# Seven products for pairs in the output projection and in the fourth quarters, with sums added by accumulating DMAs

## The chip, the cores and the metric

The kernel runs on one core of a Trainium2 chip. The metric is the device time of one execution in microseconds; for each kernel the median of several runs is given. Beside them one execution was recorded by the hardware profiler, and all rows below are of that one.

## The reference

A two-layer decoder trunk on 256 positions with model width 2048, all in float32. Each sub-layer is h = h + RMSNorm_post(f(RMSNorm_pre(h))). What matters here:

```python
def short_conv_mixer(u, w_in, conv_w, w_out):          # layer 0
    proj = u @ w_in                                     # 2048 -> 3 * 2048
    xin, gate_c, gate_b = jnp.split(proj, 3, axis=-1)
    v = gate_c * xin
    ...
    conv = sum(conv_w[k] * vp[:, k:k + S] for k in range(CONV_WIDTH))
    return (gate_b * conv) @ w_out                      # the output projection, 2048 -> 2048

def sq_relu_mlp(u, w_up, w_down):                       # after each mixer
    return jnp.square(jax.nn.relu(u @ w_up)) @ w_down   # 2048 -> 8192 -> 2048
```

Layer 0 is the gated convolution and an MLP; then one shared K and V is made; layer 1 is a stick-breaking attention with 16 heads (query projection, attention, its own output projection) and a second MLP.

## The kernel before

**Precision.** TensorE runs on float32r operands. Every float32 operand is split into a high part, rounded by ACT (`whi`, L145), and a low part, the remainder made by VectorE (`wlo`, L156). One product is then three matmuls: high with high, high with low, low with high (L282, L283, L284).

**The weight stream.** All weights come in one stream of chunks of 128x1024, 512 KB, loaded by SyncE's queue into four buffers (tag raw) and split into a ring of seven pairs of tiles (RING = 7). ACT may write the next ring tile when TensorE has finished with the one seven places earlier.

**Projections with the activations as the stationary operand.** The output projections, K, Q, V and the down projections of the MLPs work in groups of 1024 output columns. A `Group` goes over its chunks i (128 rows of the weight each) and for each chunk over two blocks b of 128 positions and two halves c of 512 columns, into four PSUM banks; a chunk is 12 matmuls of 128x512. After the last chunk the four banks are evicted. The last few chunks of a stage are taken in another order (`last_units`), so that the norm that follows can begin early.

**Seven products.** A `Mixed` group takes some neighbouring chunks i and i + 1 as a pair, a 2x2 block product by a seven-multiplication scheme. `seven` (L349 to L351) does 7 x 3 matmuls for the pair where two ordinary chunks do 8 x 3. Three products (`acc`) go straight into banks of the group; four (p1, p5, p6, p7, the tiles `more`) are kept in four further banks over all pairs of the group and combined once, after its last pair. Each pair needs

- four sums of weight blocks (`split_seven`, VectorE, L182, 128x512 each), in one tile of tag gpre with one buffer, and the split of a, b, t and u, 3.5 chunks' worth in four ring tiles, where two ordinary chunks take two;
- four sums of activation blocks (`sums_of`, L912) and their split (`two_parts`).

**The MLPs.** The hidden width is done in four quarters q. In each, `up` makes 16 hidden tiles, then two down groups j add to the results `part` (tiles `mg`). PAIRS names the pairs of each quarter and group: 2 + 2 in the fourth. In the first three quarters the four kept products are copied out by ACT (L1006) and added to the results by nine accumulating DMAs from GpSimd's queue (L998), once the group is evicted. In the fourth quarter `combined` (L1020 on) forms the four combinations in the middle of the group and VectorE adds them to the results:

```python
            def combine(p1, p5, p6, p7):
                w = pool.tile([P, 4, 512], F32, tag="gpre", name="more", bufs=1)
                t, u2, u3, u4 = (w[:, m, :] for m in range(4))
                nc.scalar.activation(t, p1[:], AF.Copy)                      # L1022
                nc.vector.tensor_tensor(u2, t, p6[:], op=ALU.add)            # L1023
                ...
                for r, v in zip(rs, (t, u4, u3, u2)):
                    nc.vector.tensor_tensor(r, r, v, op=ALU.add)             # L1029
```

At the end of the group `add` adds each bank to its result (L993) and hands it to the norm `after.post` (square on ACT, gain on VectorE at L441).

**The output projection of layer 0** follows the convolution and is two ordinary groups (`project`); their banks go to `mix0.post`. The tile gpre holds, from the stage's start, the gain row of the norm ahead of the MLP.

**What sets the order.** TensorE's order is written out by hand. VectorE, ACT and the DMA queues are ordered by a scheduler when the program is built, with some operations given priority; near the end of a stage (`begin` to `over`) VectorE's and ACT's order is also by hand. Each engine runs its queue in order: an instruction that waits holds back all behind it.

Of the kernel before, what the change touches and what calls it, by code (L numbers as in the profile page):

```python
# [14 lines left out]
P = 128  # L15
# [53 lines left out]
def trunk(ctx, tc, x, xT, vecs, rows, ws, out):  # L69
# [31 lines left out]
    def bank(i, name):  # L101
        return psum.tile([P, 512], F32, tag=f"b{i}", name=name)
# [119 lines left out]
    def part_of(xs, k, b, i):  # L222
        return xs[k // 4][:, k % 4, i, b, :]
# [152 lines left out]
    def tbank():  # L376
        turned["i"] += 1
        return bank(turned["banks"][turned["i"] % 2], "tr")


    h = [const.tile([P, D], F32, name=f"h{b}") for b in range(NB)]
# [331 lines left out]
    mlp_weights(1)  # L713


    def convolution(tmp):
        rot = {"i": -1}

# [67 lines left out]

        y = [None] * 4
        scale = {}

        mean = tmp.tile([P, P], F32, name="mean")  # L790
        nc.vector.memset(mean[:], 1.0 / D)
# [11 lines left out]
        def conv_tile(i, sx, sc, sb):  # L803
            nc.vector.tensor_tensor(sx[:], sx[:], sc[:], op=ALU.mult)
            v = tiny("v", bufs=2, cols=T + 2)
            nc.vector.memset(v[:, :2], 0.0)
            nc.vector.tensor_tensor(v[:, 2:], sx[:], scale["r2"][:], op=ALU.mult)
            c = tiny("conv", bufs=2)
            nc.scalar.activation(c[:], v[:, 2:], AF.Copy, scale=g(G_C2, i))
            nc.vector.scalar_tensor_tensor(c[:], v[:, 1 : T + 1], g(G_C1, i), c[:], op0=ALU.mult, op1=ALU.add)  # L810
            nc.vector.scalar_tensor_tensor(c[:], v[:, :T], g(G_C0, i), c[:], op0=ALU.mult, op1=ALU.add)
            nc.vector.tensor_tensor(sb[:], sb[:], scale["r"][:], op=ALU.mult)
            nc.vector.tensor_tensor(sb[:], sb[:], c[:], op=ALU.mult)
            if y[i // 4] is None:
# [58 lines left out]
    def mlp(pool, i, before, after):  # L873
# [3 lines left out]
        scale = pool.tile([P, T], F32, tag="scale", name="scale", bufs=1)  # L877
        before.spread_to = scale[:]

        def hidden(xs, n, ps, sums, pairs):  # L880
            half = pool.tile([P, T], F32, tag="half", name="half", bufs=2)
            nc.scalar.activation(half[:], ps[:, T:], AF.Copy)
            s = pool.tile([P, T], F32, tag="s", name="s", bufs=3)
            nc.vector.tensor_tensor(s[:], ps[:, :T], half[:], op=ALU.add)
            nc.vector.tensor_tensor(s[:], s[:], scale[:], op=ALU.mult)
            nc.vector.scalar_tensor_tensor(s[:], s[:], 0.0, s[:], op0=ALU.max, op1=ALU.mult)  # L886
            if xs[n // 4] is None:
                xs[n // 4] = operand("hid4")
            if n in pairs and n != APART:
                two_parts([part_of(xs, n, 0, j) for j in range(2)], s[:, :P])  # L890
            else:
                split_tile(xs, n, s[:])
            if n in pairs:
                held[n] = s
            elif n - 1 in pairs:
                sums[n - 1] = sums_of(xs, n - 1, held.pop(n - 1), s)

        def two_parts(parts, src):
            hi, lo = parts
            nc.scalar.activation(hi, src, AF.Copy)  # L900
            nc.vector.tensor_tensor(lo, src, hi.bitcast(F32), op=ALU.subtract)

        def sums_of(xs, n, x, y):

            t = after.dump()
            s1, s2, s3, s4 = (t[:, j * P : (j + 1) * P] for j in range(4))
            a11, a21, a12, a22 = x[:, :P], x[:, P:], y[:, :P], y[:, P:]
            for to, u, v, op in (
                (s1, a21, a22, ALU.add), (s2, s1, a11, ALU.subtract),
                (s3, a11, a21, ALU.subtract), (s4, a12, s2, ALU.subtract),  # L910
            ):
                nc.vector.tensor_tensor(to, u, v, op=op)  # L912
            if n == APART:
                one = pool.tile([P, 2 * P], F32R, tag="s1", name="sums", bufs=1)
                one = [one[:, j * P : (j + 1) * P] for j in range(2)]
            else:
                one = [part_of(xs, n, 1, j) for j in range(2)]
            more = pool.tile([P, 6 * P], F32R, tag="hg", name="sums", bufs=4)
            more = [more[:, j * 3 * P : (j + 1) * 3 * P] for j in range(2)]
            two_parts(one, s1)  # L920
            two_parts(more, t[:, P:])
            return one, more

        def up(q, xs, sums, pairs):
            w = W["up", i, q]
            order = UP_FIRST if q == 0 else UP_ORDER
            place = {kn: m for m, kn in enumerate(order)}
            pss = {}

            def high(k, n, b=None, begin=True, end=False):  # L930

                if n not in pss:
                    pss[n] = bank((n + 2) % 8, "up")
                ps, x = pss[n][:].rearrange("p (a b t) -> p a b t", a=2, b=NB), u[k // 4][:, k % 4]
                if b is None:
                    nc.tensor.matmul(  # L936
                        ps, weight(0, k, n), x, start=begin and k == 0, stop=end and k == KD - 1, skip_group_check=end
                    )
                else:
                    nc.tensor.matmul(ps[:, :, b, :], weight(0, k, n), x[:, :, b, :], start=k == 0 and b == 0, stop=False)  # L940
                if end and k == KD - 1:
                    hidden(xs, n, pss.pop(n), sums, pairs)
                spent(TILE_HIGH if b is None else TILE_LOW)

            def low(k, n, begin=False, end=True):
                if n not in pss:
                    pss[n] = bank((n + 2) % 8, "up")
                x = u[k // 4][:, k % 4, 0].rearrange("p b t -> p (b t)")
                nc.tensor.matmul(  # L949
                    pss[n][:, :T], weight(1, k, n), x, start=begin and k == 0, stop=end and k == KD - 1,  # L950
                    skip_group_check=begin,
                )
                if end and k == KD - 1:
                    hidden(xs, n, pss.pop(n), sums, pairs)
# [62 lines left out]
        def combined(j):  # L1017

            def combine(p1, p5, p6, p7):
# [6 lines left out]
                nc.vector.tensor_tensor(u2, u3, p5[:], op=ALU.add)  # L1026
                rs = [part[b][2 * j + c] for b in range(NB) for c in range(2)]
                for r, v in zip(rs, (t, u4, u3, u2)):
                    nc.vector.tensor_tensor(r, r, v, op=ALU.add)  # L1029
            return combine  # L1030

        for q in range(QUARTERS):
# [21 lines left out]
    def sublayer_pool(name, post, pre):  # L1054
        pool = tc.alloc_tile_pool(name=name, bufs=1, reuse_waits="tile")
        return pool, Norms(pool, row(pool, post, "gpost"), row(pool, pre, "gpre"))
# [262 lines left out]
```

## Time and profile before

| | |
|---|---|
| median of 3 runs | 2144.81 us (2144.78 to 2145.4) |
| the profiled execution | 2144.68 us |
| its span, first to last instruction | 2143.0 us |
| mean granted TensorE clock | 0.999 |
| TensorE busy | 2132.1 us, 99% |
| VectorE, ACT, GpSimd busy | 1649.2, 1241.1, 100.1 us |
| DMA | 445.55 MB, mean 208 GB/s |

The span is what the rows cover; the execution's own time is a little longer. In a row, a line such as L182 is a line of the kernel before; `out<-in` are the tiles written and read; PE is TensorE, DVE is VectorE, POOL is GpSimd. In a row of the timeline the first two numbers are start and duration in microseconds, and brackets tell how long the engine was idle before it and what released it.

### The profile page before, as it was taken

The numbers are of one execution on the slowest core, as the hardware profiler recorded it, in microseconds if no ns is written. First come the engines' busy times: TensorE is split into PE (matmuls) and PEld (weight loads), VectorE is DVE, ScalarE is ACT, GpSimd is POOL, SyncE is SP. The second block draws the span as 40 slices with busy tenths as digits, with TensorE's granted clock in tenths as the row PEclk, the third lists the DMA queues.
The fourth block names the chain that finished last, engine by engine and source line by source line (L and its number), as shares of the span: only waits on it lengthen the run. The fifth ranks groups of instructions, "written<-read, shape, count | busy, mean of one in ns | idle before, by whom it ended". The sixth has DMA issues, their size and how long they took to land.

```text
span 2143.0 us, 29715 instructions
## 1 busy us (share of the span) xinstructions
PE 2132.1 (99%) x10926; PEld 1825.7 (85%) x10926; DVE 1649.2 (77%) x2475; ACT 1241.1 (58%) x1748; POOL 100.1 (5%) x121
## 2 busy tenths in 40 slices
PE   9999999999999999999999999999999999999998
PEld 8888888888888888888888888889888888888886
DVE  7766655898788789678866777558987896887787
ACT  7545444656556556555567888446565565555544
POOL 0000000001101101100000000000011011011000
PEclk9999999999999999999999999999999999999999
DMA  8655664669858858965575545655688588579763
GB/s 305 217 189 186 192 232 146 198 196 263 246 171 255 256 167 245 281 192 175 176 227 166 157 158 177 215 159 167 200 256 259 170 244 267 187 205 268 228 197 124
DMA packets 130321, 445.55 MB, mean 208 GB/s; under 512 B 14592, under 2 KB 14848, under 8 KB 129152
## 3 DMA queue, kind: packets, MB, share of 16 engines
q1 hardware_dynamic: 113472, 408.65, 58.6%
q0 software_dynamic: 16416, 34.61, 8.4%
q8 instruction: 86, 1.41, 0.3%
q14 instruction: 59, 0.48, 0.1%
q10 hardware_dynamic: 288, 0.39, 0.1%
HBM read 413.19 MB, written 2.10 MB: 194 GB/s over the span
## 4 chain that ended last, share of the span: by engine, by line
PE 98%; ACT 1%; DMA 1%; DVE 0%; issue 0%; SPq 0%; DVEq 0%; ACTq 0%
PE up L936 21%; PE acc L282 13%; PE acc L284 13%; PE acc L283 13%; PE up L949 11%; PE acc L758 11%; PE more L350 2%; PE more L349 2%; PE more L351 2%; PE acc L350 2%; PE acc L349 2%; PE acc L351 2%; PE lead L758 1%; PE up L940 1%; PE tr L235 1%; PE z L1092 0%
## 5 line engine op out<-in xcount | busy, mean ns | idle before, releaser
L156 DVE TENSOR_TENSOR wlo<-raw,whi 128x1024 fp32r<-128x1024 f32 (+1 forms) x574 | 687.7, 1211 | 299.5 <-ACT whi L145 244.0
L145 ACT ACTIVATE whi<-raw 128x1024 fp32r<-128x1024 f32 (+1 forms) x574 | 598.1, 1048 | 314.6 <-PE acc L284 135.7
L936 PE MATMUL up<-u,whi 128*128 128x512 f32 x1952 | 458.9, 390 | 0.5 <-ACT scale L517 0.5
L936 PEld LDWEIGHTS up<-u,whi 128*128 128x128 f32 x1952 | 361.6, 188 | 72.3 <-ACT scale L517 0.7
L949 PEld LDWEIGHTS up<-u,wlo 128*128 128x128 f32 x2048 | 256.0, 191 | 5.8
L949 PE MATMUL up<-u,wlo 128*128 128x256 f32 x2048 | 259.0, 283 | 0.0
L282 PE MATMUL acc<-whi,hid 128*128 128x512 f32 x608 | 236.6, 389 | 0.0
L284 PE MATMUL acc<-whi,hid 128*128 128x512 f32 x608 | 236.5, 389 | 0.0
L283 PE MATMUL acc<-wlo,hid 128*128 128x512 f32 x608 | 236.5, 389 | 0.0
L158 DVE SCALAR_TENSOR_TENSOR wlo<-raw,gv,whi 128x512 fp32r<-128x512 f32 (+1 forms) x160 | 132.1, 854 | 42.0 <-ACT whi L145 41.4
L758 PE MATMUL acc<-u,whi 128*128 128x512 f32 x672 | 156.5, 390 | 0.0
L282 PE MATMUL acc<-whi,u 128*128 128x512 f32 x384 | 153.1, 399 | 0.3 <-ACT tk L1162 0.3
L145 ACT ACTIVATE whi<-raw,gv 128x512 fp32r<-128x512 f32 (+1 forms) x160 | 121.8, 800 | 51.8 <-PE acc L284 32.5
L284 PE MATMUL acc<-whi,u 128*128 128x512 f32 x384 | 149.9, 390 | 0.0
L283 PE MATMUL acc<-wlo,u 128*128 128x512 f32 x384 | 149.7, 390 | 0.0
L758 PEld LDWEIGHTS acc<-u,whi 128*128 128x128 f32 x672 | 124.8, 188 | 25.0
L282 PEld LDWEIGHTS acc<-whi,hid 128*128 128x128 f32 x608 | 114.1, 188 | 23.7
L284 PEld LDWEIGHTS acc<-whi,hid 128*128 128x128 f32 x608 | 114.1, 188 | 23.7
L283 PEld LDWEIGHTS acc<-wlo,hid 128*128 128x128 f32 x608 | 114.1, 188 | 23.6
L229 ACT ACTIVATE hid<-s 128x256 fp32r<-128x256 f32 x106 | 44.2, 417 | 135.5 <-DVE s L886 135.1
L998 POOL DMA_DIRECT2D mg<-more x96 | 84.3, 984 | 280.1 <-DMA mg<-more 170.0
L284 PEld LDWEIGHTS acc<-whi,u 128*128 128x128 f32 x384 | 72.1, 188 | 15.4
(2720 smaller groups left out, 3125.3 us busy)
## 6 DMA issues: line engine op xcount, KB each, us to landing
raw<-w_up SPq DMA_DIRECT2D x256, 512.0 KB, 4.5
raw<-w_dn SPq DMA_DIRECT2D x256, 512.0 KB, 4.4
raw<-w_in SPq DMA_DIRECT2D x94, 512.0 KB, 4.0
mg<-more POOLq DMA_DIRECT2D x96, 256.0 KB, 7.4
raw<-w_out SPq DMA_DIRECT2D x32, 512.0 KB, 3.6
raw<-w_v SPq DMA_DIRECT2D x32, 512.0 KB, 4.4
raw<-w_k SPq DMA_DIRECT2D x32, 512.0 KB, 4.3
raw<-w_q SPq DMA_DIRECT2D x32, 512.0 KB, 4.0
```

What stands on the lines that cost most here:

```text
L145: rounded = nc.scalar.activation(hi[:, at], raw[i][:, at], AF.Copy, scale=1.0 if gain is None else gain)
L156: nc.vector.tensor_tensor(lo[:, at], t[:, at], hi[:, at].bitcast(F32), op=ALU.subtract)
L158: nc.vector.scalar_tensor_tensor(lo[:, at], t[:, at], gain, hi[:, at].bitcast(F32), op0=ALU.mult, op1=ALU.subtract)
L282: nc.tensor.matmul(ps[:], xh, hi[:, a], start=i == 0 and k == 0, stop=False)
L283: nc.tensor.matmul(ps[:], xh, lo[:, a], start=False, stop=False)
L284: nc.tensor.matmul(ps[:], xl, hi[:, a], start=False, stop=i == self.n - 1 and k == self.ks - 1)
L349: nc.tensor.matmul(ps[:], xh, hi, start=own and i == self.pairs[0], stop=False)
L350: nc.tensor.matmul(ps[:], xh, lo, start=False, stop=False)
L351: nc.tensor.matmul(ps[:], xl, hi, start=False, stop=own and i == self.pairs[-1])
L758: nc.tensor.matmul(ps[:, :cols], w, xs[:, :cols], start=k == 0 and part == parts[0], stop=k == KD - 1 and part == parts[1], skip_group_che ...
L936: nc.tensor.matmul(ps, weight(0, k, n), x, start=begin and k == 0, stop=end and k == KD - 1, skip_group_check=end)
L949: nc.tensor.matmul(pss[n][:, :T], weight(1, k, n), x, start=begin and k == 0, stop=end and k == KD - 1, skip_group_check=begin,)
```

## The change

Three things are done.

1. The first group of layer 0's output projection becomes a `Mixed` group with the pairs 4, 8 and 11 (chunks 4-5, 8-9, 11-12). The convolution keeps the tiles of y that form a pair and makes their sums (`sums_of`, `two_parts`), in tiles of tag mg. The new `seven_out` combines p1, p5, p6, p7 into the four result tiles after pair 11 (one copy on ACT, four additions on VectorE), and its eviction adds each bank to the result that exists already. The gain row in gpre is loaded only at the start of the second group, since the weight sums of the pairs use that tile.
2. In the fourth quarter of each MLP the pairs are (2, 4, 8) in the first group and (2, 4) in the second, where both had (2, 6). A pair that only the first group has keeps its tile whole ("apart"), as chunk 11 did before; in the first quarter, where both groups have 11, it is no longer treated so.
3. In `combined` the four additions onto the results on VectorE become four accumulating DMAs from GpSimd's queue.

`two_parts`, `sums_of` and `halves` move to the kernel's top level.

```diff
-PAIRS = ([(2, 5, 8, 11)] * 2, [(2, 5, 8, 11), (2, 5, 8)], [(2, 5, 8, 11), (2, 5, 8)], [(2, 6)] * 2)
-APART = 11
+PAIRS = ([(2, 5, 8, 11)] * 2, [(2, 5, 8, 11), (2, 5, 8)], [(2, 5, 8, 11), (2, 5, 8)], [(2, 4, 8), (2, 4)])
+OUT_PAIRS = (4, 8, 11)
...
     def convolution(tmp):
...
             split_tile(y, i, sb[:])
+            if i in OUT_PAIRS:
+                held[i] = sb
+            elif i - 1 in OUT_PAIRS:
+                t = tmp.tile([P, 2 * T], F32, tag="sq", name="sq", bufs=1)
+                sums_of(t, held.pop(i - 1), sb)
+                parts = [res.tile([P, 512], F32R, tag="mg", name="sums") for _ in range(2)]
+                two_parts([p[:] for p in parts], t[:])
+                out_sums[i - 1] = [p[:, :P] for p in parts], [p[:, P:] for p in parts]
...
-        def hidden(xs, n, ps, sums, pairs):
+        def hidden(xs, n, ps, sums, pairs, apart):
...
-            if n in pairs and n != APART:
+            if n in pairs and n not in apart:
...
         def combined(j):
...
                 rs = [part[b][2 * j + c] for b in range(NB) for c in range(2)]
                 for r, v in zip(rs, (t, u4, u3, u2)):
-                    nc.vector.tensor_tensor(r, r, v, op=ALU.add)
+                    nc.gpsimd.dma_start(r, v, accum_op=ALU.add)
             return combine
...
-            up(q, xs, sums, pairs[0])
+            up(q, xs, sums, pairs[0], set(pairs[0]) - set(pairs[1]))
...
+    def seven_out(w, xs, norms, pool):
+
+        part = [[None] * 2 for _ in range(NB)]
+
+        def combine(p1, p5, p6, p7):
+            (t, u4), (u3, c22) = part[:] = [[result() for _ in range(2)] for _ in range(NB)]
+            u2 = norms.dump()[:]
+            nc.scalar.activation(t, p1[:], AF.Copy)
+            for to, x, ps in ((u2, t, p6), (u3, u2, p7), (u4, u2, p5), (c22, u3, p5)):
+                nc.vector.tensor_tensor(to, x, ps[:], op=ALU.add)
+
+        def evict(b, c, ps):
+            r = part[b][c]
+            with tc.high_priority():
+                nc.vector.tensor_tensor(r, r, ps[:], op=ALU.add)
+            norms.post(b, c, r, r)
+
+        return Mixed(w.base, xs, [[0, 1], [2, 3]], evict, out_sums, [4, 5, 6, 7], combine, pool, OUT_PAIRS)
 
     turned["banks"] = [0, 1]
-    pool0, mix0 = sublayer_pool("p_mlp0", B_POST0, B_MLP0)
-    run(project(W["out"], y, 2, sublayer(mix0)), leave=mix0)
+    pool0, mix0 = sublayer_pool("p_mlp0", B_POST0)
+    groups = [seven_out(W["out"], y, mix0, pool0), project(W["out"], y, 2, sublayer(mix0))[1]]
+
+    def last_gain():
+        mix0.gpre = row(pool0, B_MLP0, "gpre")
+
+    groups[1].start = last_gain
+    run(groups, leave=mix0)
```

More of the change, by code (lines that the diff above doesn't have):

```diff
@@ L378, in tbank, with two_parts, sums_of, halves @@
         return bank(turned["banks"][turned["i"] % 2], "tr")
+    def two_parts(parts, src):
+        hi, lo = parts
+        nc.scalar.activation(hi, src, AF.Copy)
+        nc.vector.tensor_tensor(lo, src, hi.bitcast(F32), op=ALU.subtract)
+    def sums_of(t, x, y):
+        (a11, a21), (a12, a22) = halves(x), halves(y)
+        s1, s2, s3, s4 = (t[:, j * P : (j + 1) * P] for j in range(4))
+        for to, u, v, op in (
+            (s1, a21, a22, ALU.add), (s2, s1, a11, ALU.subtract),
+            (s3, a11, a21, ALU.subtract), (s4, a12, s2, ALU.subtract),
+        ):
+            nc.vector.tensor_tensor(to, u, v, op=op)
+    def halves(t):
+        return [t[:, j * P : (j + 1) * P] for j in range(2)]
     h = [const.tile([P, D], F32, name=f"h{b}") for b in range(NB)]
@@ L713, in trunk @@
     mlp_weights(1)
+    out_sums = {}
     def convolution(tmp):
@@ L788, in convolution @@
         scale = {}
+        held = {}
         mean = tmp.tile([P, P], F32, name="mean")
@@ L895, in hidden, with up @@
             elif n - 1 in pairs:
[L896 to L924, printed above, removed]
+                x = held.pop(n - 1)
+                if n - 1 in apart:
+                    one = halves(pool.tile([P, T], F32R, tag="s1", name="sums", bufs=1))
+                else:
+                    one = [part_of(xs, n - 1, 1, j) for j in range(2)]
+                more = pool.tile([P, 6 * P], F32R, tag="hg", name="sums", bufs=4)
+                more = [more[:, j * 3 * P : (j + 1) * 3 * P] for j in range(2)]
+                t = after.dump()
+                sums_of(t, x, s)
+                two_parts(one, t[:, :P])
+                two_parts(more, t[:, P:])
+                sums[n - 1] = one, more
+        def up(q, xs, sums, pairs, apart):
             w = W["up", i, q]
@@ L941, in high @@
                 if end and k == KD - 1:
-                    hidden(xs, n, pss.pop(n), sums, pairs)
+                    hidden(xs, n, pss.pop(n), sums, pairs, apart)
                 spent(TILE_HIGH if b is None else TILE_LOW)
@@ L953, in low @@
                 if end and k == KD - 1:
-                    hidden(xs, n, pss.pop(n), sums, pairs)
+                    hidden(xs, n, pss.pop(n), sums, pairs, apart)
                 spent(TILE_LOW)
@@ L1050, in mlp, with sublayer_pool @@
                 turned["banks"] = [2, 3]
-            up(q, xs, sums, pairs[0])
+            up(q, xs, sums, pairs[0], set(pairs[0]) - set(pairs[1]))
             run(groups, leave=after if last else None)
-    def sublayer_pool(name, post, pre):
+    def sublayer_pool(name, post, pre=None):
         pool = tc.alloc_tile_pool(name=name, bufs=1, reuse_waits="tile")
-        return pool, Norms(pool, row(pool, post, "gpost"), row(pool, pre, "gpre"))
-    turned["banks"] = [0, 1]
-    pool0, mix0 = sublayer_pool("p_mlp0", B_POST0, B_MLP0)
-    run(project(W["out"], y, 2, sublayer(mix0)), leave=mix0)
+        return pool, Norms(pool, row(pool, post, "gpost"), None if pre is None else row(pool, pre, "gpre"))
+    def seven_out(w, xs, norms, pool):
[12 more added lines that the diff above has]
+        return Mixed(w.base, xs, [[0, 1], [2, 3]], evict, out_sums, [4, 5, 6, 7], combine, pool, OUT_PAIRS)
+    turned["banks"] = [0, 1]
+    pool0, mix0 = sublayer_pool("p_mlp0", B_POST0)
[4 more added lines that the diff above has]
+    run(groups, leave=mix0)
     kv = KeyNorms(pool0, None)
```

## The prediction

> **What bounds the kernel now.** I read the page first: shares by engine, clock, and the chain that ended last.
>
> ```profile
> span 2143.0 us, 29715 instructions
> PE 2132.1 (99%) x10926; PEld 1825.7 (85%) x10926; DVE 1649.2 (77%) x2475; ACT 1241.1 (58%) x1748; POOL 100.1 (5%) x121
> PEclk9999999999999999999999999999999999999999
> PE 98%; ACT 1%; DMA 1%; DVE 0%; issue 0%; SPq 0%; DVEq 0%; ACTq 0%
> ```
>
> The reader is to see that TensorE is busy for 99% of the span at full clock, and that 98% of the chain is its own. Next, the waits of TensorE alone:
>
> ```profile
> PE warm L748 <- DVE ones L86: 1.1, 1, 1.1
> PE up L936 <- ACT scale L517: 0.5, 1, 0.5
> PE acc L282 <- ACT tk L1162: 0.3, 1, 0.3
> ```
>
> Three waits in all, 1.9 us together, none in a down projection or in the output projection. So the time is the number of matmuls times their pitch, plus a head and a tail, and a change can only win by removing matmuls and only lose by making TensorE wait. The groups give 389 ns for one matmul of 128x512, but matmuls overlap, so I take the pitch from the timeline of a pair in the last quarter (first MLP):
>
> ```profile
> 983.27 0.39 PE L349 MATMUL more<-whi358a,hid 128*128 128x512 f32 x1
> ...
> 987.81 0.39 PE L351 MATMUL acc<-whi358u,hid 128*128 128x512 f32 x1
> 988.03 0.39 PE L282 MATMUL acc<-whi,hid 128*128 128x512 f32 x1
> ```
>
> From 983.27 to 988.03 a pair issues 7 x 3 = 21 matmuls: 4.76 us, 0.2267 us each. An ordinary chunk is 4 x 3 = 12 of them, 2.72 us, so a pair done with eight products would take 5.44 us.
>
> **The sum.** The profiled execution took 2144.68 us, its span 2143.0 and 1.68 around it; the median of the runs shown is 2144.81. Each new pair saves one product, three matmuls, 0.68 us.
>
> - Output projection, three pairs: 9 matmuls, -2.04 us.
> - Fourth quarters: two pairs and two become three and two, one more in each MLP: 6 matmuls, -1.36 us. The changed program lists 15 matmuls fewer, which agrees.
>
> Together -3.40 us, if TensorE never waits for what replaces them. That is the part to check.
>
> **What a pair costs VectorE, and what covers it.** Rows of VectorE while a pair of weights is split (four sums L182, then low parts of a, b, t, u at L156):
>
> ```profile
> 1016.16 0.69 DVE L182 TENSOR_TENSOR sums<-raw 128x512 f32<-128x512 f32 x1
> 1016.77 0.69 DVE L182 TENSOR_TENSOR sums<-raw,raw 128x512 f32<-128x512 f32 x1
> ...
> 1019.18 1.22 DVE L156 TENSOR_TENSOR wlo374b<-raw,whi374b 128x1024 fp32r<-128x1024 f32 x1
> 1020.31 1.22 DVE L156 TENSOR_TENSOR wlo374t<-sums,whi374t 128x1024 fp32r<-128x1024 f32 x1
> ...
> 1022.58 1.22 DVE L156 TENSOR_TENSOR wlo<-raw,whi 128x1024 fp32r<-128x1024 f32 x1
> ```
>
> The pitch is 0.60 us for a 512-wide operation and 1.13 for a 1024-wide one; the whole pair takes 1016.16 to 1022.58, 6.42 us, against 4.76 us of TensorE. Two ordinary chunks cost 2.26, so a new pair adds 4.16. VectorE therefore loses 1.66 us on TensorE in each pair and lives on its lead: seven split tiles, which ACT refills when TensorE has read them. How much room the stages have:
>
> ```profile
> 273.70:317.30 43.60, 43.60 (x194) 36.11 (x193) 22.09 (x22) 19.13 (x23) 1.24 (x2) 1.00 0.71 241
> 967.60:1009.80 42.20, 42.20 (x188) 34.92 (x187) 35.08 (x43) 21.85 (x25) 0.00 (x0) 1.00 0.63 200
> ```
>
> These are the windows of the output projection's first group and of a fourth quarter's first group (behind the length stand busy time and count of TensorE, weight loads, VectorE, ACT and POOL). In the output projection VectorE goes from 22.1 to 22.1 + 3 x 4.16 + 8 x 0.60 (four adds of the combination, four evictions onto results that exist already) = 39.4 of 41.6 us. It fits, and two ordinary chunks stand between the pairs 4 and 8 to rebuild the lead. If the cover failed, each pair would show its 1.66 us, 5.0 us for three; I take 0, because the stage begins with four ordinary chunks, in which VectorE, half idle in this row, fills all seven tiles. The row gpre, now loaded at the start of the second group, has nearly all of that group (16 chunks, 43.5 us) to land. The sums of y cost VectorE 4 small operations and a low part a pair, within a convolution without a wait in the table above: 0.
>
> In the fourth quarter's first group the pairs 2 and 4 now touch. Before, the second pair's last low part came here:
>
> ```profile
> 977.82 1.22 DVE L156 TENSOR_TENSOR wlo358u<-sums,whi358u 128x1024 fp32r<-128x1024 f32 x1
> ```
>
> It was done at 979.0, with TensorE at that pair from 983.27. Two chunks earlier means 977.83, its u part wanted 15 matmuls later, at 981.2; and two ordinary low parts that stood ahead of it now stand behind. Done by about 977, it is 4 us early: 0. The busy time becomes 35.1 + 4.2 - 2.4 (four adds gone) = 36.9 of 41.5. The adds taken off VectorE (16 of 0.60) were never on the chain, so their going is worth 0 as well. The first quarters' shorter split of chunk 11 likewise: 0.
>
> **The new wait.** The four sums of a combination lie in one tile (tag gpre), and so do the weight sums of every pair. Before, VectorE itself read them; now four DMAs do, and in the changed program's listing the first weight sum of the second group's pair 2 waits on four semaphores of software DMAs. It stands in VectorE's in-order queue ahead of all later low parts and of the first group's evictions. Count from T, the end of the first group's last pair (988.03 in the row above). The combination before:
>
> ```profile
> 984.49 0.58 ACT L1022 ACTIVATE more<-more 128x512 f32<-128x512 f32 x1
> 985.76 0.69 DVE L1029 TENSOR_TENSOR mg<-mg,more 128x512 f32<-128x512 f32 x1
> 987.50 0.68 DVE L1023 TENSOR_TENSOR more<-more 128x512 f32<-128x512 f32 x1
> 990.42 0.69 DVE L1029 TENSOR_TENSOR mg<-mg,more 128x512 f32<-128x512 f32 x1
> 991.03 0.68 DVE L1026 TENSOR_TENSOR more<-more 128x512 f32<-128x512 f32 x1
> ```
>
> Its last sum (L1026) ended at T + 3.7; without the add of 990.42, but with one more low part in the order before it, I take T + 3.5. Then POOL issues the last DMA. DMAs of just this kind and size are in the trace, 96 of them; the first two lines are all of them, the others two bursts of three at the start of a second group, with a short and a long last landing:
>
> ```profile
> L998 POOL DMA_DIRECT2D mg<-more x96: 860/870/1952, 494.9 to 1986.0; - x96
> DMA to landing us min/median/max: 3.5/7.4/13.1
> ...
> L998 POOL DMA_DIRECT2D mg<-more x3: 869/925/1288, 838.3 to 839.7; - x3
> DMA to landing us min/median/max: 3.9/6.0/6.8
> ...
> L998 POOL DMA_DIRECT2D mg<-more x3: 869/921/1284, 1749.2 to 1750.6; - x3
> DMA to landing us min/median/max: 4.4/6.2/8.7
> ```
>
> Ours is the third of such a burst, so I take 7 us: VectorE is let go at T + 10.6 (bounds T + 7.0 by 3.5, T + 16.6 by 13.1). What follows it includes the evictions:
>
> ```profile
> 1007.95 0.69 DVE L993 TENSOR_TENSOR mg<-mg,acc 128x512 f32<-128x512 f32 x1 [1.03 <-PE acc L284]
> 1008.56 1.22 DVE L156 TENSOR_TENSOR wlo370u<-sums,whi370u 128x1024 fp32r<-128x1024 f32 x1
> ...
> 1012.09 1.89 DVE L441 TENSOR_TENSOR mg<-mg,gpost 128x512 f32<-128x512 f32 x3
> 1013.89 2.36 DVE L156 TENSOR_TENSOR wlo<-raw,whi 128x1024 fp32r<-128x1024 f32 x2
> ```
>
> That block, with the low part u in it, took 5.94 us. So, in the changed order: four sums 2.40, low parts b and t 2.26, the block 5.94, then of the next pair (4) four sums and a 3.00, b 1.13. That low part b is ready 14.7 us after the release, at T + 25.3. TensorE wants it after six chunks, two chunks, a whole pair and four matmuls: 16.32 + 5.44 + 4.76 + 0.91 = T + 27.4. It is the tightest of the parts. The slack is 2.1 us; TensorE waits once the last DMA lands later than T + 12.7, that is 9.2 us after its issue. Cost taken: 0 us; bounds 0 and 2 x (16.6 - 12.7) = 7.8 us, and not below nothing, since a wait cannot shorten the matmuls behind it.
>
> The Trainium skill, page "DMA: Bandwidth & Descriptors", section "Anatomy of one DMA", fits a DMA of this path with 2.0 us plus bytes over 436 GB/s, for 256 KB an estimate of 2.6 us. By it the release would be near T + 6 and the rival below would have no chance; the trace's median of 7.4 us does not agree, and the trace decides.
>
> The page "SBUF — State Buffer", section "SBUF: two separate sides", speaks against the move: descriptors of DMAs issued from GpSimd starve while VectorE is in a two-port mode. It infers that two-input operations, which fill VectorE here, do not do this. In this kernel the mechanism would be longer issues on POOL: three at the longest of the row above, 1.95 instead of 0.87 us, would move the release by 3.2 us to T + 13.8 and cost 2 x 1.1 = 2.2 us, 2143.6 us in all. The median of the issues, 870 ns beside a busy VectorE, shows no such stretch; I count it to the partial form of the first rival.
>
> The results that the DMAs add to are next touched by evictions: in the first group after five and a quarter chunks, T + 14.3; in the second group, counted from its own last pair, after four ordinary chunks and six half units of 0.68 us, T + 15 at the earliest: the DMA of the first result, issued ahead of the sums, has landed by then. The end of the kernel is untouched:
>
> ```profile
> 2134.45 0.69 DVE L993 TENSOR_TENSOR mg<-mg,acc 128x512 f32<-128x512 f32 x1 [1.48 <-PE acc L284]
> ```
>
> VectorE waits there for the last matmul, so the tail simply moves forward with it.
>
> **Forecast.** 2144.68 - 3.40 = 2141.28; on the median's footing 2141.4 us, 0.16% down. About 0.2%, 4.3 us, is what a measurement of this kernel can tell from no change, so this counts as the same.
>
> **Rivals.**
> - *The DMAs land late, and the time ends on the slower side.* Place: VectorE in front of the weight sums of the second group's first pair, in both MLPs. It begins to cost at T + 12.7 and undoes the saving at T + 14.4 (1.7 us in each MLP). At the longest landing, 13.1 us, it costs 7.8 us: 2141.4 + 7.8 = 2149.2, slower by 0.2%. For it: 13.1 did occur among the 96. Against: the bursts shown, at the same place of other quarters, end at 6.8 and 8.7. A partial form, 1 to 4 us in all, gives 2142.4 to 2145.4. Chances 0.07 full, 0.12 partial.
> - *The lead fails in the output projection.* VectorE at 39.4 of 41.6 us falls behind and shows 1.66 us in each of three pairs: 2141.4 + 5.0 = 2146.4, no gain. For it: the share. Against: the lead built in the first four chunks. Chance 0.06.
> - *More is gained than counted.* TensorE is busy 2132.1 of 2143.0 us; 8.55 of the 10.9 idle are the tail behind 2134.45 and 1.1 the first wait of the table, so 1.25 us lie within the run. If VectorE and ACT, ordered anew, gave all of it back: 2141.4 - 1.25 = 2140.15, just past the 0.2% mark (2140.5). Against: the waits named there do not stand near the edits. Chance 0.07.
>
> **How the numbers follow.** The forecast has 0.68. Range: from the third rival's 2140.2 to the end of the partial form, 2145.4; left out are the full form and the second rival, 0.13. Faster by over 0.2%: 0.07, the third rival. Slower by over 0.2% (above 2149.1): 0.07 for the late DMAs in full and 0.02 for a failed lead together with partly late DMAs, 0.09. Within: 0.84.
>
> **What would show it.** Right: 15 matmuls fewer at the same pitch; no wait of TensorE in the windows of the output projection or the fourth quarters; VectorE idle for some 4 us ahead of the weight sums of the second group's first pair, released by a DMA of mg; that DMA landing 5 to 9 us after issue. Wrong: a gap of TensorE before a low part of the second group's pairs (late DMAs), or before low parts of the output projection's pairs (lead), or a pitch other than 0.2267 us.

## The result and the profile after

The changed kernel took 2153.6 us (median; 2152.24 to 2155.83), the kernel before 2144.97 beside it; ratio 1.0042, 95% interval 1.0027 to 1.0056. It is slower, by 8.6 us, where 3.4 us of gain were forecast. The profiled execution took 2155.63 us, its span 2153.9. The page's head, and TensorE's waits:

```profile
span 2153.9 us, 29783 instructions
...
PE 2134.9 (99%) x10911; PEld 1825.0 (85%) x10911; DVE 1672.1 (78%) x2524; ACT 1252.9 (58%) x1766; POOL 114.1 (5%) x137
...
PE 92%; DMA 3%; DVE 3%; ACT 1%; issue 1%; DVEq 0%; SPq 0%; ACTq 0%
```

```profile
PE tr L235 <- DVE h L541: 2.8, 1, 2.8
PE acc L282 <- ACT whi L145: 1.9, 2, 1.2
PE acc L283 <- DVE wlo L156: 1.9, 3, 0.8
...
PE acc L350 <- DVE wlo372b L156: 0.8, 1, 0.8
PE acc L350 <- DVE wlo756b L156: 0.8, 1, 0.8
```

15 matmuls fewer, as the sum said. But "PE 99%" hides a loss: the idle time grew from 10.9 to 19.0 us, which still rounds to 99%, and a matmul that runs at a lower clock counts as busy. It is the chain that shows it, where TensorE's share fell from 98 to 92%, and the wait table, which had no row of a down projection before. But for 1.0 us at the start (in a row left out here), all new waits lie in the second groups of the two fourth quarters and right behind them; there is none in the output projection.

VectorE ahead of the second group (first MLP; the first group's last pair ends at T = 991.17, where the next matmul starts in the second fence), and the chain through the same group:

```profile
994.39 0.68 DVE L1041 TENSOR_TENSOR more<-more 128x512 f32<-128x512 f32 x1
...
1004.72 0.69 DVE L182 TENSOR_TENSOR sums<-raw 128x512 f32<-128x512 f32 x1 [4.71 <-DMA mg<-more]
```

```profile
991.17 0.39 PE L282 MATMUL acc<-whi,hid 128*128 128x512 f32 x1
```

```profile
995.37 9.22 DMA mg<-more
...
1018.55 1.14 DVE wlo372b L156
...
1025.39 6.33 DMA raw<-w_dn
...
1034.15 8.22 DMA raw<-w_v
```

The last of the four DMAs is issued at T + 4.2 and lands 9.2 us later; VectorE, idle for 4.71 us, goes on at T + 13.5. The chain, which left TensorE at the combination, runs from there over VectorE and late loads of raw weights to the end of the MLP. TensorE's own rows show the price:

```profile
1018.57 0.40 PE L349 MATMUL acc<-whi372b,hid 128*128 128x512 f32 x1
1019.74 0.50 PE L350 MATMUL acc<-wlo372b,hid 128*128 128x512 f32 x1 [0.77 <-DVE wlo372b L156]
...
1042.08 0.39 PE L282 MATMUL acc<-whi,hid 128*128 128x512 f32 x1
1043.09 0.50 PE L283 MATMUL acc<-wlo,hid 128*128 128x512 f32 x1 [0.62 <-DVE wlo L156]
...
1049.61 0.39 PE L284 MATMUL acc<-whi,hid 128*128 128x512 f32 x1
1052.83 0.66 PE L235 MATMUL tr<-ident,h 128*128 128x128 f32 x4 [2.84 <-DVE h L541]
...
1053.56 0.57 PE L283 MATMUL acc<-wlo,hid 128*128 128x512 f32 x1
...
1056.91 0.45 PE L282 MATMUL acc<-whi,u 128*128 128x512 f32 x1
```

From start to start, less one pitch of 0.23: 0.94, 0.78 and 2.99 us; then 8 matmuls in 3.35 us, 0.42 each, 1.5 us too long: 6.2 us in the first MLP. The second, at its end:

```profile
2124.68 0.39 PE L284 MATMUL acc<-whi,hid 128*128 128x512 f32 x1
2126.26 0.49 PE L282 MATMUL acc<-whi,hid 128*128 128x512 f32 x1 [1.19 <-ACT whi L145]
2127.52 0.50 PE L283 MATMUL acc<-wlo,hid 128*128 128x512 f32 x1 [0.77 <-DVE wlo L156]
2127.86 0.40 PE L284 MATMUL acc<-whi,hid 128*128 128x512 f32 x1
2128.95 0.79 PE L282 MATMUL acc<-whi,hid 128*128 128x512 f32 x1 [0.69 <-ACT whi L145]
2130.20 0.79 PE L283 MATMUL acc<-wlo,hid 128*128 128x512 f32 x1 [0.47 <-DVE wlo L156]
2130.80 0.63 PE L284 MATMUL acc<-whi,hid 128*128 128x512 f32 x1
...
2135.49 0.47 PE L283 MATMUL acc<-wlo,hid 128*128 128x512 f32 x1
```

Gaps of 1.35, 1.03, 0.86, 1.03 and 0.37 us, then 11 matmuls in 4.69 us, 2.2 too long; with some 0.9 for the gap at wlo756b of the table, 7.8 us. Both MLPs: 14.0 us lost against 3.4 saved, and the span is 10.9 longer.

### The profile page after: what moved, and what is told of

Read it like the earlier page. It is cut to its first block, busy times and chain, and to the rows that moved or that the text cites. A ratio compares the mean times of both kernels' runs of the same rounds, so it can differ in the third digit from the quotient of the medians.

```text
span 2153.9 us, 29783 instructions
## 1 busy us (share of the span) xinstructions
PE 2134.9 (99%) x10911; PEld 1825.0 (85%) x10911; DVE 1672.1 (78%) x2524; ACT 1252.9 (58%) x1766; POOL 114.1 (5%) x137
## 4 chain that ended last, share of the span: by engine, by line
PE 92%; DMA 3%; DVE 3%; ACT 1%; issue 1%; DVEq 0%; SPq 0%; ACTq 0%
PE up L951 21%; PE up L964 11%; PE acc L284 11%; PE acc L283 11%; PE acc L282 11%; PE acc L779 11%; PE more L351 2%; PE more L349 2%; PE more L350 2%; PE acc L351 2%; PE acc L349 2%; PE acc L350 2%; PE lead L779 2%; DMA raw<-w_dn 1%; PE up L955 1%; DMA mg<-more 1%
## 5 line engine op out<-in xcount | busy, mean ns | idle before, releaser
L156 DVE TENSOR_TENSOR wlo<-raw,whi 128x1024 fp32r<-128x1024 f32 (+1 forms) x564 | 675.1, 1210 | 277.4 <-ACT whi L145 223.0
L145 ACT ACTIVATE whi<-raw 128x1024 fp32r<-128x1024 f32 (+1 forms) x564 | 587.2, 1048 | 296.5 <-PE acc L284 102.2
L282 PE MATMUL acc<-whi,hid 128*128 128x512 f32 x592 | 232.3, 392 | 1.9 <-ACT whi L145 1.9
L284 PE MATMUL acc<-whi,hid 128*128 128x512 f32 x592 | 232.0, 392 | 0.0
L158 DVE SCALAR_TENSOR_TENSOR wlo<-raw,gv,whi 128x512 fp32r<-128x512 f32 (+1 forms) x160 | 132.0, 853 | 40.2 <-ACT whi L145 39.5
L912 ACT ACTIVATE half<-up 128x256 f32<-128x256 f32 x128 | 48.1, 380 | 64.5 <-PE up L951 35.3
```

Source lines behind the costliest of these rows:

```text
L145: rounded = nc.scalar.activation(hi[:, at], raw[i][:, at], AF.Copy, scale=1.0 if gain is None else gain)
L156: nc.vector.tensor_tensor(lo[:, at], t[:, at], hi[:, at].bitcast(F32), op=ALU.subtract)
L158: nc.vector.scalar_tensor_tensor(lo[:, at], t[:, at], gain, hi[:, at].bitcast(F32), op0=ALU.mult, op1=ALU.subtract)
L282: nc.tensor.matmul(ps[:], xh, hi[:, a], start=i == 0 and k == 0, stop=False)
L284: nc.tensor.matmul(ps[:], xl, hi[:, a], start=False, stop=i == self.n - 1 and k == self.ks - 1)
```

## The experiments

Each result is the median with its ratio to the kernel before, run beside it on the same chip (2144.2 to 2144.5 us there), and the 95% interval.

**Which part of the change costs.** Three kernels undo parts of it. The theory was that the accumulating DMAs are the cause; the rival, the touching pairs 2 and 4, which load VectorE.

```diff
 e1:        nc.gpsimd.dma_start(r, v, accum_op=ALU.add)  ->  nc.vector.tensor_tensor(r, r, v, op=ALU.add)
 e3:        last entry of PAIRS [(2, 4, 8), (2, 4)]  ->  [(2, 6)] * 2
 e4:        both of these; only the output projection's pairs are left
```

> The changed kernel with all its pairs, but the four sums of a combination added on VectorE again. Theory (the accumulating DMAs cause the loss): all 15 matmuls are saved and nothing else changes, 2141.0 to 2142.5 us, no wait of TensorE for a low part of weights in the second groups of the fourth quarters. Rival (the pairs 2 and 4 that touch, with 4.16 us more of VectorE each, eat the lead): 2149 to 2154 us, with the gaps before low parts still there.

Measured: 2142.44 us, ratio 0.9991 (0.9982 to 0.9999).

> The changed kernel with the fourth quarters' pairs back at 2 and 6 in both groups; the sums still added by DMAs. 6 matmuls more than the changed kernel, the sum alone gives 2142.9 us. Theory (the DMAs cause the loss, by the wait on their tile and by late loads): VectorE idles 3 to 5 us ahead of the second group's first weight sums in each MLP; pair 6 instead of 4 gives 5.4 us more room, so the loss is smaller but not gone, 2144 to 2149 us. Rival (the touching pairs): no gap, 2142.5 to 2143.3 us.

Measured: 2143.41 us, 0.9998 (0.9989 to 1.0006), a loss of 1.2 against e4, which has the same matmuls. This is less than the theory expected, and just above the range of the rival.

> Only the output projection's three pairs are left of the change; fourth quarters with pairs 2 and 6 and sums added on VectorE, as before. Both theories: 9 matmuls less, 2.04 us, 2142.5 to 2143.3 us. If the three pairs themselves cost something (the lead fails, or the start is longer, as the profile of the changed kernel has 1.4 us more ahead of its first matmuls): 2144 to 2146 us.

Measured: 2142.2 us, 0.9988 (0.998 to 0.9997).

With the adds on VectorE the loss is gone, so the DMAs are needed for it. But they are not enough: with pairs 2 and 6 they cost 1.2 us, with 2, 4, 8 they cost 11 to 12 (the two runs of the changed kernel against e1). And e1 has six matmuls less than e4, 1.36 us, and is no faster. Where these went, by TensorE's waits in e1, and by VectorE at the end of the first MLP in e1 and then in e4:

```profile
PE tr L235 <- DVE h L541: 1.4, 2, 1.3
```

```profile
1042.53 1.28 DVE L158 SCALAR_TENSOR_TENSOR wlo<-raw,gv,whi 128x1024 fp32r<-128x1024 f32 x1 [1.20 <-ACT whi L145]
1043.73 0.68 DVE L1008 TENSOR_TENSOR mg<-mg,acc 128x512 f32<-128x512 f32 x1
```

```profile
1041.31 1.29 DVE L158 SCALAR_TENSOR_TENSOR wlo<-raw,gv,whi 128x1024 fp32r<-128x1024 f32 x1 [1.09 <-ACT whi L145]
1042.51 0.68 DVE L1008 TENSOR_TENSOR mg<-mg,acc 128x512 f32<-128x512 f32 x1
```

In VectorE's queue the low parts of the next stage's weights (L158) stand ahead of the evictions (L1008) on which the transposes wait. In e1 they come 1.2 us later than in e4, and TensorE stands in front of the transposes for 1.3 us instead of 0.2.

**Which DMAs, and the wait or the traffic.** The changed kernel again, then the DMAs in one group alone (a condition on j around the line above, adds on VectorE in the other), then the sums in a tile that no weight sum uses.

```diff
 e7:  DMAs if j == 0          e6:  DMAs if j == 1
 e5:  w = pool.tile([P, 4, 512], F32, tag="gpre", ...)  ->  w = act.tile([P, 4, 512], F32, tag="x4", ...)
 e14: e5 and e7 together
```

> The changed kernel once more, beside the others on one chip. Both theories: 2150 to 2156 us, with gaps of TensorE in front of low parts of weights in the second groups of both fourth quarters and a longer one in front of the transposes that follow the first MLP.

Measured: 2154.89 us, 1.0041 (1.0027 to 1.0055).

> The changed kernel with the sums of the fourth quarter's second group added on VectorE; those of the first group by DMAs as changed. Theory (the wait of the weight sums on the first group's DMAs is the main cause): the idle time of VectorE of 3 to 5 us and the gap at the low part b of pair 4 stay, the loss is smaller by the collision of the second group's DMAs with loads only: 2146 to 2152 us. Rival (the second group's DMAs, which meet the loads that are catching up, are the main cause): 2142 to 2144.5 us.

Measured: 2152.49 us, 1.0033 (1.002 to 1.0045): 10.0 us above e1.

> The changed kernel with the sums of the fourth quarter's first group added on VectorE; those of the second group by DMAs as changed. Theory (the wait on the first group's DMAs is the main cause): no idle time of VectorE ahead of weight sums, 2142.4 us of the kernel with all adds on VectorE plus 0 to 2 us for slower loads: 2142 to 2144.5 us. Rival (the second group's DMAs are the main cause): 2147 to 2152 us.

Measured: 2144.25 us, 0.9996 (0.9987 to 1.0004): 1.8 above e1.

> The changed kernel, but the sums of the fourth quarters' combinations lie in a tile of the operands' ring, which is free there, and no longer in the tile that the weight sums of the pairs use: the DMAs stay, the wait of the weight sums on them goes. If that wait is the cause: VectorE's idle time of 4.7 us ahead of the weight sums is gone, 2141 to 2143.5 us. If the DMAs harm by slowing the loads of raw weights (landing 6 to 8.5 us where 3.4 to 5.4 were seen before): loads still late, 2145 to 2151 us.

Measured: 2144.89 us, 1.0003 (0.9994 to 1.0012): 2.4 above e1.

> The sums of the fourth quarter's first group added by four DMAs, from a tile of their own, so that no weight sum waits on them; the second group's on VectorE. The kernel with the same four DMAs in the tile of the weight sums took 2152.5 us. Theory (the wait costs, the traffic little): 2142 to 2144.5 us. Rival (the traffic of the first group's DMAs delays the loads that the second group lives on): 2147 to 2152 us.

Measured: 2144.8 us, 1.0002 (0.9994 to 1.0011): 2.4 above e1.

Without the shared tile both kernels are a little above what was expected for them (2143.5 and 2144.5 us at most), and far below the changed kernel. The first group's DMAs cost 10.0 us with the shared tile and 2.4 without: 7.6 us by the wait; the other 2.4 I put down to the traffic. VectorE's waits in e7 and in e14:

```profile
DVE sums L182 <- DMA mg<-more: 4.1, 1, 4.1
```

```profile
DVE sums L182 <- DMA raw<-w_dn: 1.9, 1, 1.9
```

Without the tile's wait VectorE still waits, for raw weights. The DMA table of 987 to 1000 us, in the kernel before and in the changed kernel (landing in us at the end of the row; the queues' share is of 16 engines):

```profile
raw<-w_dn SPq DMA_DIRECT2D x7, 512.0 KB, 5.0
```

```profile
q1 hardware_dynamic: 763, 2.80, 63.0%
q0 software_dynamic: 389, 0.73, 30.7%
...
raw<-w_dn SPq DMA_DIRECT2D x6, 512.0 KB, 6.6
mg<-more POOLq DMA_DIRECT2D x4, 256.0 KB, 7.9
```

Both kinds share the engines, and both land later. The traffic of the two groups does not seem to add up (2.4 and 1.8 us apart, 2.4 together), but the runs of e5 and of e6 scatter over some 4 us each, so this is open.

**One DMA in place of four.** Only the first sum of the first group, or only the last, by a DMA.

```diff
 e12: DMA if j == 0 and v is t          e11: DMA if j == 0 and v is u2
```

> Of the fourth quarters' eight sums a MLP only the first of the first group (the plain copy of p1, ready before the pair ends) is added by a DMA; seven by VectorE. In the trace of the changed kernel that DMA lands about 9 us after 988.5, when the sums are just finished. Theory (what costs is how late the weight sums' tile is let go): the wait of VectorE is below 1.5 us, 2142 to 2144 us. Rival (any accumulating DMA in that place costs its share, a quarter of the 10 us that the four cost): 2144.5 to 2146 us.

Measured: 2142.56 us, 0.9991 (0.9982 to 1.0).

> Of the fourth quarters' eight sums a MLP only the last of the first group (the one that is ready last) is added by a DMA; seven by VectorE. Theory (how late the tile is let go): the DMA is issued about when the fourth was in the changed kernel and, with less traffic beside it, lands 5 to 8 us later; VectorE, which now has 1.8 us of adds to do in between, idles 2 to 4 us, TensorE has its gaps at low parts of pair 4: 2146 to 2152 us. Rival (cost by the number of DMAs): 2144.5 to 2146 us.

Measured: 2142.46 us, 0.999 (0.9981 to 0.9999). Expected was 2146 to 2152, so the expected landing was wrong, and the rival's share of the cost did not show either. VectorE and the DMA table of e11:

```profile
995.04 3.49 DVE L156 TENSOR_TENSOR wlo<-raw,whi 128x1024 fp32r<-128x1024 f32 x3
998.45 0.69 DVE L182 TENSOR_TENSOR sums<-raw 128x512 f32<-128x512 f32 x1
```

```profile
raw<-w_dn SPq DMA_DIRECT2D x6, 512.0 KB, 4.5
mg<-more POOLq DMA_DIRECT2D x1, 256.0 KB, 3.5
```

As the only one of its group, the same DMA lands in 3.5 us, loads take 4.5, and VectorE goes from its low parts straight into the first weight sum. Loads run beside it here too, so the 9.2 us of the changed kernel come with the other three DMAs.

**Where the combination and the next pair stand.** All sums by DMAs, three and two pairs as changed, at other places.

```diff
 last entry of PAIRS [(2, 4, 8), (2, 4)]  ->  e10: [(2, 6, 10), (2, 6)]   e18: [(2, 6, 8), (2, 6)]   e19: [(2, 4, 6), (2, 4)]
```

> The changed kernel with the fourth quarters' pairs at 2, 6, 10 and 2, 6 instead of 2, 4, 8 and 2, 4; all eight sums by DMAs as changed, in the tile of the weight sums. As many products and as much work for VectorE. Theory (VectorE's idle time costs only as far as the second group's next pair is near: two ordinary chunks more are 5.4 us more room and 3.2 us more of lead): VectorE idles 3 to 5 us as before, few gaps of TensorE in the second group, 2143 to 2146 us. Rival (VectorE's load in the group as such is too high for the idle time): 2149 to 2154 us.

Measured: 2153.81 us, 1.0045 (1.0031 to 1.0059). The edit did more than meant: pair 10 moves the combination 5.4 us nearer to the second group's weight sums. So the next two:

> The changed kernel with the pairs 2, 6, 8 and 2, 6 instead of 2, 4, 8 and 2, 4; all sums by DMAs in the tile of the weight sums, combination after the same chunk. Theory A (what counts is the room up to the second group's next pair): the wait of VectorE stays 4 to 5 us, no gap at the low part b of the next pair, 2143 to 2147 us. Theory B (what is late at the weight sums stays late up to the end of the MLP, wherever the next pair stands): 2149 to 2154 us, with the gap in front of the transposes.

Measured: 2150.05 us, 1.0025 (1.0016 to 1.0034).

> The changed kernel with the pairs 2, 4, 6 and 2, 4 instead of 2, 4, 8 and 2, 4: as many products, the second group's pairs still touch, all sums by DMAs in the tile of the weight sums, but the combination stands two chunks (5.4 us) earlier. Theory (what counts is when the tile is let go before the second group's weight sums): VectorE idles less than 2 us on it, 2142.5 to 2146 us. Rival (touching pairs and the DMAs' traffic as such): 2150 to 2154 us.

Measured: 2150.76 us (2146.56 to 2154.26), 1.0027 (1.0018 to 1.0036).

e18, VectorE's wait and TensorE's:

```profile
DVE sums L182 <- DMA mg<-more: 5.5, 1, 5.5
```

```profile
PE tr L235 <- DVE h L541: 4.8, 1, 4.8
```

With the next pair two chunks later the gap at its low part is gone, and TensorE waits 4.8 us in front of the transposes instead. So theory B holds in the first MLP: what is late at the weight sums is late at its end. VectorE's rows show the way:

```profile
1045.69 1.28 DVE L158 SCALAR_TENSOR_TENSOR wlo<-raw,gv,whi 128x1024 fp32r<-128x1024 f32 x1 [1.39 <-ACT whi L145]
1046.89 0.68 DVE L1008 TENSOR_TENSOR mg<-mg,acc 128x512 f32<-128x512 f32 x1
```

TensorE did not wait for weights in this group, but the first eviction comes at 1046.89 instead of e4's 1042.51, behind a low part of the next stage that waited for its load. In the second MLP no stage follows. There VectorE waited 4.6 us for the same DMA, and TensorE's gaps are only 0.75 and 0.49 us, so theory A holds there. No run puts the low parts of the next stage behind the evictions.

e19, VectorE's waits of 960 to 1062 us, and the table of 987 to 1000:

```profile
DVE wlo L156 <- ACT whi L145: 13.3, 9, 2.3
```

```profile
raw<-w_dn SPq DMA_DIRECT2D x6, 512.0 KB, 6.9
```

No wait on a DMA of mg is left, as expected, and yet 8.3 us are lost against e1: as I read it, three pairs in a row use up the lead, and loads at 6.9 us can't restore it; the stall comes in nine pieces behind ACT, which itself waits for weights. My theory fell here: letting the tile go in time is not enough while VectorE has no lead. No kernel with these pairs and the adds on VectorE was run, so what the touching pairs cost and what the DMAs cost can't be told apart; and the profiled execution, 2153.25 us, is one of the longest of its kernel. e3 shows the other side: its first weight sum waited 4.2 us too, for a load, and began at 999.2; it lost 1.2 us; VectorE has one pair less to split there, and the combination stands as early as in e19.

**Pairs without DMAs.** Adds on VectorE, pairs spread; then in the second MLP alone; then with one DMA.

```diff
 e8:  e1 with the last entry of PAIRS [(2, 6, 10), (2, 6)]
 e13: e8 with  pairs = PAIRS[q] if i or not last else [(2, 6)] * 2
 e15: e13 with the last sum of the first groups by a DMA, as in e11
```

> All adds on VectorE, and the fourth quarters' pairs at 2, 6, 10 and 2, 6 instead of 2, 4, 8 and 2, 4: as many products, two ordinary chunks between pairs. The kernel with all adds on VectorE and touching pairs took 2142.44 us and its trace has one wait of 1.3 us in front of the transposes after the first MLP. Theory (VectorE's work for the touching pairs is late there): the wait goes, 2140.5 to 2141.6 us. Rival (the wait comes from the added pair or from the removed matmuls themselves, wherever the pairs stand): 2142 to 2143 us.

Measured: 2142.02 us, 0.9986 (0.9977 to 0.9995); the wait is 0.9 us instead of 1.3, and the time lies in the rival's range: most of the wait is there wherever the pairs stand.

> All adds on VectorE; pairs at 2, 6, 10 and 2, 6 in the fourth quarter of the second MLP only, at 2 and 6 in both groups of the first. Theory (in the first MLP the added pair's saving of 0.68 us is eaten by the wait of 0.9 to 1.3 us in front of the transposes behind it, in the second it is kept): 2141.2 to 2141.8 us, no wait over 0.4 us after the first MLP. Rival (the saving is kept in neither MLP): 2142.0 to 2142.6 us, as with the pairs of both MLPs or of none (2142.0, 2142.2).

Measured: 2141.47 us, 0.9987 (0.9978 to 0.9996), 0.7 below e4; the wait is gone:

```profile
PE warm L769 <- DVE ones L86: 1.1, 1, 1.1
PE acc L282 <- ACT tk L1202: 0.3, 1, 0.3
PE lead L779 <- ACT whi L145: 0.2, 1, 0.2
```

> The kernel with the added pairs in the second MLP only (2141.47 us), and the last sum of the first groups by a DMA, the form that lost nothing (2142.46 us with touching pairs in both MLPs). Theory: VectorE loses one add, which was not on the chain: the same as without it, 2141.0 to 2141.9 us. Rival (VectorE's backlog at the end of the group is worth its 0.6 us): 2140.4 to 2141.0 us.

Measured: 2141.92 us, 0.9989 (0.9981 to 0.9998): no gain from one add less, within the scatter of e13.

So, by these medians, an added pair earns its 0.68 us in the second MLP and nothing in the first. e13 beats both kernels: 0.13% below the kernel before.

**The slow matmuls behind the gaps.** Matmuls on ones ahead of the transposes keep TensorE busy in the longest gap.

```diff
+        for _ in range(filler.pop() if filler else 0):
+            nc.tensor.matmul(to[:, :P], ones[:], ones[:], start=True, stop=True)
 e16: filler 24 in the first MLP          e17: 11
```

> The changed kernel, with 24 matmuls of 128x128 on ones added ahead of the transposes behind the first MLP, where TensorE was idle for 3 us; they write what the transposes overwrite. Theory (the eight matmuls at 427 ns behind that gap, 0.2 us each too long, come from the idle time itself): they take 227 ns, 1.0 to 1.6 us less, 2152.0 to 2153.9 us beside the changed kernel's 2153.6 and 2154.9. Rival (the half pitch comes from something else, such as late weights): the 427 ns stay, 2153.6 to 2155 us.

Measured: 2155.97 us, 1.0058 (1.0046 to 1.0071). The added work took 5.5 us, twice what I had allowed for, and so made TensorE late itself.

> The changed kernel with 11 matmuls of 128x128 on ones ahead of the transposes behind the first MLP; in e16 24 of them took 5.5 us, so these take 2.5 of the 3.0 us in which TensorE idled. Theory (the half pitch behind the gap comes from the idle time): the eight matmuls at 427 ns go, 1.0 to 1.6 us less than the changed kernel's 2153.6 and 2154.9: 2151.9 to 2153.9 us. Rival: no change, 2153.6 to 2155 us.

Measured: 2153.82 us, 1.0044 (1.003 to 1.0058), which by the time alone parts nothing. The rows of the windows do, 1053 to 1057 us in the changed kernel and in e17 (behind the counts of the engines stand the granted clock, the DMA share and GB/s):

```profile
1053.00:1057.00 4.00, 4.00 (x14) 3.21 (x14) 1.72 (x3) 2.25 (x4) 0.00 (x0) 0.58 0.00 0
```

```profile
1053.00:1057.00 4.00, 4.00 (x20) 3.28 (x19) 3.37 (x9) 2.62 (x6) 0.00 (x0) 1.00 0.00 0
```

Granted clock 0.58 and 14 matmuls against 1.00 and 20: the slow stretch comes from TensorE having idled. In e16, too, the clock behind the added matmuls (1055 to 1059 us) is 1.00. The span of e17's profiled execution is 2152.0 us, against 2153.9 and 2153.2 of the changed kernel's two, but the medians do not show it: how much of the time these slow matmuls are worth is not settled.

## Why the prediction was wrong

**The sum** held where TensorE sets the pace. Output projection: -2.04 forecast, -2.1 measured (e4). Second MLP: -0.68, and -0.7 (e13 against e4). First MLP: -0.68, and nothing.

**What a pair costs VectorE, and what covers it.** Right for the output projection (no wait in it in the changed kernel), and right that the removed adds are worth 0 (e11 and e15 against e1 and e13). Wrong at the fourth quarter of the first MLP: I looked for cover at the pair itself, and never asked what VectorE does last in the group. There the evictions stand behind the next stage's low parts, and the extra 4.16 us of VectorE come out as 0.9 to 1.3 us in front of the transposes (e8, e1).

**The new wait** is the step that failed, in three places.
- The landing: I took 7 us from bursts of three, measured were 9.2. Ours was the fourth of its group; as the only one it landed in 3.5 us (e11). The last sum ended at T + 3.9 instead of T + 3.5, too, and its DMA was issued at T + 4.2. Release at T + 13.5 instead of T + 10.6, beyond my limit of T + 12.7.
- The price behind the limit: by my working, 0.8 us beyond it cost 0.8 in each MLP, 1.7 us in all. At that place it was right: low part b was ready at 1019.7, T + 28.5, and TensorE lost 0.94 us at just that matmul. But I took the tightest part for the only price. From 1005 to 1030 us VectorE was busy for 25.0 of 25.0 us, so nothing rebuilt the lead; from 1030 to 1046 us it was busy for half of the time and waited for loads (the row below, with the DMA engines at 0.93). The same lateness was charged again at the late chunks and at the transposes: 6.2 and 7.8 us instead of 0.8 in each MLP. In e18, with two ordinary chunks more before the next pair, the low part had no gap; 4.8 us came at the end of the first MLP, 1.2 in the second.
- The side effects: I set the DMAs' effect on loads at nothing. What is left without the wait is 2.4 us in e14, and 1.8 in e6, which is hardly clear of the scatter; how much of e19's 8 us is theirs is open. And gaps made the matmuls behind them slow, 3.7 of the 14.0 us.

```profile
1030.00:1046.00 16.00, 15.38 (x68) 12.35 (x68) 8.50 (x8) 8.58 (x8) 0.87 (x1) 1.00 0.93 295
```

The first rival named the mechanism and the place; its largest size, 7.8 us, was too small, for the first two of these reasons. The second rival did not occur. The page "DMA: Bandwidth & Descriptors", section "Anatomy of one DMA", of the Trainium skill, whose estimate of 2.6 us I set aside for the median of 7.4, comes nearer to the DMA that is the only one of its group, 3.5 us in e11, though this is 0.9 us more. What had to be priced was the other DMAs beside it.

## What to carry to other kernels

Moving work from an engine that is 77% busy to DMAs does not free it if it then waits for them: before you put a consumer behind a DMA, look up which tile tag it shares with later work and what stands behind it in that engine's queue, up to the end of the stage. A helper engine's load has to be read in the stage's own window, and its room is set by its last duty there, not by the nearest part. A stall of an engine without a lead is paid again at each later place that waits for it, up to the end of the stage, unless the work in between gives the lead back, as in e18's second MLP: price it there, not once.

## What the chip showed that was not expected

- Transfers in each other's way. A 256 KB accumulating DMA within the SBUF landed in 3.5 us alone and in 9.2 as the fourth of a group; loads of 512 KB beside it went from 5.0 to 6.6 us (medians). By the queue rows above, the accumulating DMAs took 30.7% of the engines' time for 0.73 MB, the loads 63.0% for 2.80: about 1.9 times as much for each byte.
- Half pitch after idling. Behind the gap of 3.0 us, and behind 4.6 us of gaps spread over 6.1, matmuls started every 0.42 us instead of 0.23, at granted clocks of 0.58 and, in 2131 to 2136 us, 0.54. Single gaps of 1.4 us (e1) and 1.9 us (e7) left the pitch alone, one of 2.8 us (e14) did not. The Trainium skill, page "TensorE: Matmul & The Clock Gate", section "What's actually happening", tells of half clock after a free-running window of about 3.4 us of idling; the rate agrees, but here single gaps of 2.8 and 3.0 us were enough. The second MLP's gaps, none over 1.35 us, show that several short ones bring it about as well: the matmul at 2128.95, behind three gaps of 3.2 us together, already took 0.79 us instead of 0.39.

```profile
2131.00:2136.00 5.00, 5.00 (x13) 3.88 (x13) 1.76 (x5) 0.72 (x2) 0.00 (x0) 0.54 0.00 0
```
